# Mixture-of-experts stages: whole fp32 matmuls on unsplit weights, expert pairs in the two column halves of TensorE

## The chip, the cores and the metric

The kernel runs on one core of a Trainium2 chip. The metric is the time of one execution on the device in microseconds (us). Three runs of the kernel before gave 2243.08, 2245.78 and 2247.37 us; the median is 2245.78.

The engines go by the names of the profile: PE is TensorE (PEld its weight loads), DVE is VectorE, ACT is ScalarE, POOL is GpSimd, SP issues most transfers from memory.

## The reference, cut to what matters

A block of two layers comes first (a gated delta rule mixer, then an attention mixer), and behind each mixer stands a mixture of experts over 256 tokens of width 1024. A second block follows, which the change doesn't touch. The part that the change is about:

```
def hier_moe(x, w_grp, b_grp, w_rt, b_rt, w_gate, w_up, w_down):
    ...                                  # softmax over 4 groups, best group; in it the best 2 of 4 experts
    gate = jnp.sum(jax.nn.one_hot(expert_id, MOE_EXPERTS, dtype=jnp.float32) * top_w[..., None], axis=1)
    def step(acc, e_in):
        wg, wu, wd, ge = e_in            # 1024 x 256, 1024 x 256, 256 x 1024, all float32
        hdn = jax.nn.silu(xt @ wg) * (xt @ wu)
...
    y, _ = lax.scan(step, jnp.zeros((b * t, d), jnp.float32), (w_gate, w_up, w_down, gate.T))
```

In the sum over 16 experts a token counts only for the two that it was routed to. Each layer has its own 16 experts, 50.3 MB of weights.

## The kernel before

Activations stand as h: 128 partitions x 8 blocks (kb) x 256 tokens. Weights are one long array W in the order of use; `load` streams it in pieces of 128x1024 (512 KB) into `wraw` buffers (5) through SP. Products are made in fp32r, which needs the operands cut in two: `fill` copies each piece to a rounded high part `wh` (ACT, L161) and subtracts for the low part `wl` (L164, columns up to `s.cut` on DVE, the rest on POOL), and `mm3` (L184 to L186) multiplies high by high, high by low and low by high.

One expert stage, `moe`, runs so. The norm of the mixer ahead ends with transposes of its statistics (L229 on `ln_st`), then writes h and its two parts `xh`, `xl`. Expert 0 is computed for all tokens: `dense_in` with `mm3`, gate and up together, 256 columns each. Meanwhile the router's logits (L832) are formed, DVE works out the routing, and `places` gives each routed token one of CAP = 64 slots in its expert's list. `gather` (L941) multiplies the tokens (`XT`, high and low) by one-hot matrices (`OH`), and leaves each expert's list as 64 columns high and 64 low.

Experts 1 to 15 then go one at a time through a loop: `gate_up` (L1026) holds the list's 128 columns (high, low) in the array and streams the weights' high and low parts, 512 columns each; `hidden` adds the two halves by a matmul with `fold` (L1044) and makes silu(gate) x up; `down` (L1058) does the second product the same way; `combine` (L1072) brings a result back to token order with a selection matrix (`Sel`), 256 columns, and `put_back` adds it to h. At the end `begin` and `end` do expert 0's second product with `mm3` and the last combines, pair by pair, for the norm that follows. `m_cnt` guards a branch (L1087) for lists of over 64 tokens, which isn't taken here.

Around the loop `room` and `again` lend `load` five more buffers of 512 KB (the space of xh and xl, and one tile `more_w`). A scheduler orders the instructions of each engine from the program and its priorities.

## Time and profile before

| | us |
|---|---|
| median of 3 runs | 2245.78 |
| the profiled execution, its own time | 2242.31 |
| its span, first to last instruction | 2240.4 |
| PE busy | 2108.0 (94%) |
| DVE busy | 1563.2 (70%) |
| ACT, POOL busy | 1194.7, 1204.8 |
| expert stage of layer 0, statistics to statistics | 231.64 to 458.68 |
| expert stage of layer 1 | 631.24 to 855.68 |

The span is the profiled execution's time without some 2 us around it. An engine's busy time is a sum over stages of different kinds, so what a change in the expert stages is worth is to be read in these two stretches, which are a fifth of the span.

### The profile page before, as it was taken

To read this page: it belongs to the slowest core of one execution; us is meant where nothing else is said; L and a number is where in the kernel's file an instruction comes from. 1 tells how busy PE (TensorE), PEld (TensorE's weight loads), DVE (VectorE), ACT (ScalarE), POOL (GpSimd) and SP (SyncE) were. 2 spreads that over 40 slices of the span, in tenths; PEclk is the share of its full clock that TensorE was granted. 3 is DMA by queue.
4 is the path that set the end of the run, shared out by engine and by line. 5 is a ranking of instruction groups with operands and counts; after the bars stand their busy time and mean duration, and the time that the engine had idled before them with its cause. 6 is when DMAs were issued, how large, how long until landed. Compare 5 with 4: busy or idle time off the path is not lost.

```text
span 2240.4 us, 43315 instructions
## 1 busy us (share of the span) xinstructions
PE 2108.0 (94%) x16219; PEld 1994.8 (89%) x16219; DVE 1563.2 (70%) x2995; ACT 1194.7 (53%) x2036; POOL 1204.8 (54%) x1100
## 2 busy tenths in 40 slices
PE   8899899889989988999899999999999989999998
PEld 8889777788787777999899999999999988999998
DVE  6856799767779986664788656664665688656654
ACT  6723588556557764444565544444444466545443
POOL 3513466444245655776624367556676644367663
PEclk9999799889989998999999999999999999999999
DMA  5413388553047864555333355555555432355553
GB/s 199 142 37 108 123 284 297 192 182 122 22 146 262 290 236 135 194 175 175 127 104 118 115 175 168 173 176 173 170 178 172 164 109 92 117 184 176 187 186 107
DMA packets 111911, 363.53 MB, mean 162 GB/s; under 512 B 21064, under 2 KB 25160, under 8 KB 111304
## 3 DMA queue, kind: packets, MB, share of 16 engines
q1 hardware_dynamic: 107400, 354.82, 47.7%
q10 hardware_dynamic: 4288, 5.80, 0.8%
q8 instruction: 132, 2.16, 0.4%
q14 instruction: 91, 0.75, 0.1%
HBM read 359.13 MB, written 1.44 MB: 161 GB/s over the span
## 4 chain that ended last, share of the span: by engine, by line
PE 43%; DVE 4%; POOL 2%; ACT 1%; issue 1%; POOLq 0%; DVEq 0%; ACTq 0%
PE bankg L184 13%; PE bankg L185 13%; PE bankg L186 13%; PE bank L1833 2%; PE bank L1757 1%; DVE wl L164 1%; POOL rms_acc L1518 1%; PE bank L1818 1%; ACT wh L161 1%; POOL wl L164 1%; ACT x_p L1741 0%; POOL sq L1516 0%; DVE x_p L1730 0%; DVE x_p L1750 0%; PE bank L1784 0%
## 5 line engine op out<-in xcount | busy, mean ns | idle before, releaser
L164 POOL TENSOR_TENSOR wl<-wraw,wh 128x256 fp32r<-128x256 f32 (+4 forms) x560 | 741.6, 1327 | 603.9 <-ACT wh L161 507.4
L161 ACT ACTIVATE wh<-wraw 128x1024 fp32r<-128x1024 f32 x560 | 590.7, 1058 | 516.9 <-PE bankg L185 260.6
L184 PE MATMUL bankg<-xh,wh 128*128 128x272 f32 (+1 forms) x2624 | 770.0, 294 | 16.0 <-ACT wh L161 7.5
L185 PE MATMUL bankg<-xl,wh 128*128 128x272 f32 (+1 forms) x2624 | 761.3, 290 | 8.1 <-DVE xl L1524 4.3
L186 PE MATMUL bankg<-xh,wl 128*128 128x272 f32 (+1 forms) x2624 | 762.1, 291 | 0.8 <-DVE wl L164 0.7
L164 DVE TENSOR_TENSOR wl<-wraw,wh 128x768 fp32r<-128x768 f32 (+3 forms) x544 | 560.9, 1034 | 267.9 <-ACT wh L161 266.7
L184 PEld LDWEIGHTS bankg<-xh,wh 128*128 128x128 f32 x2624 | 505.2, 193 | 24.8 <-ACT wh L161 7.5
L185 PEld LDWEIGHTS bankg<-xl,wh 128*128 128x128 f32 x2624 | 505.2, 193 | 11.0 <-DVE xl L1524 5.9
L186 PEld LDWEIGHTS bankg<-xh,wl 128*128 128x128 f32 x2624 | 505.5, 193 | 2.1 <-DVE wl L164 1.3
L186 PE MATMUL bankg<-f_hh,wl 128*128 128x272 f32 (+1 forms) x704 | 201.4, 286 | 0.0
L184 PE MATMUL bankg<-f_hh,wh 128*128 128x272 f32 (+1 forms) x704 | 201.2, 286 | 0.0
L185 PE MATMUL bankg<-f_hl,wh 128*128 128x272 f32 (+1 forms) x704 | 200.8, 285 | 0.0
L184 PEld LDWEIGHTS bankg<-f_hh,wh 128*128 128x128 f32 x704 | 132.6, 188 | 0.0
L185 PEld LDWEIGHTS bankg<-f_hl,wh 128*128 128x128 f32 x704 | 132.5, 188 | 0.0
L186 PEld LDWEIGHTS bankg<-f_hh,wl 128*128 128x128 f32 x704 | 132.2, 188 | 0.0
L1574 POOL TENSOR_TENSOR f_g<-f_g,f_u 128x272 f32<-128x272 f32 (+1 forms) x88 | 69.8, 793 | 82.6 <-DVE f_u L1573 80.9
L1573 DVE TENSOR_TENSOR f_u<-bankg,rb 128x272 f32<-128x272 f32 (+1 forms) x88 | 38.4, 437 | 82.3 <-PE bankg L186 82.3
L233 DVE TENSOR_TENSOR f_hl<-f_g,f_hh 128x272 fp32r<-128x272 f32 (+1 forms) x88 | 83.0, 943 | 4.4 <-ACT f_hh L232 4.4
L1026 PE MATMUL bankg<-wl,m_xg 128*128 128x512 f32 x240 | 78.1, 407 | 2.6 <-DVE wl L164 2.4
L1026 PE MATMUL bankg<-wh,m_xg 128*128 128x512 f32 x240 | 79.6, 413 | 0.5 <-DVE m_xg L948 0.5
L164 POOL TENSOR_TENSOR wl<-more_xl,wh 128x320 fp32r<-128x320 f32 x40 | 46.5, 1169 | 30.5 <-ACT wh L161 23.3
L164 POOL TENSOR_TENSOR wl<-more_xh,wh 128x320 fp32r<-128x320 f32 x40 | 45.0, 1126 | 32.8 <-ACT wh L161 29.6
(584 smaller groups left out, 4081.6 us busy)
## 6 DMA issues: line engine op xcount, KB each, us to landing
wraw<-W SPq DMA_DIRECT2D x560, 512.0 KB, 3.6
more_xl<-W SPq DMA_DIRECT2D x40, 512.0 KB, 4.8
more_xh<-W SPq DMA_DIRECT2D x40, 512.0 KB, 4.7
more_w<-W SPq DMA_DIRECT2D x20, 512.0 KB, 6.2
bt<-rpb SPq DMA_DIRECT2D x8, 544.0 KB, 6.3
n_tb<-t ACTq DMA_DIRECT2D x1, 2048.0 KB, 8.1
n_c<-cmp_k ACTq DMA_DIRECT2D x1, 1024.0 KB
n_c<-cmp_v ACTq DMA_DIRECT2D x1, 1024.0 KB
```

What stands on the lines that cost most here:

```text
L161: nc.scalar.activation(wh, r, AF.Copy)
L164: eng.tensor_sub(wl[:, sl], r[:, sl], wh[:, sl].bitcast(F32))
L184: mm(out, wh, xh, start=start, stop=False, **k)
L185: mm(out, wh, xl, start=False, stop=False, **k)
L186: mm(out, wl, xh, start=False, stop=stop, **k)
L233: s.nc.vector.tensor_sub(l, x, h.bitcast(F32))
L1026: PE.matmul(GUs[e], XG[(e - 1) // 4][:, k0 + i, (e - 1) % 4], ws[i][part], start=k0 + i + part == 0, stop=k0 + i + part == KB)
L1518: nc.gpsimd.tensor_add(st["acc"], st["acc"], sq)
L1573: V.tensor_mul(u, pu, rb)
L1574: G.tensor_mul(g, g, u)
L1757: PE.transpose(pt[:96, b * 128:(b + 1) * 128], p[:, b * 96:(b + 1) * 96], s.ident)
L1833: PE.matmul(o[hf * 64:hf * 64 + 64, c * 128:(c + 1) * 128], v(j)[:, b, hf * 64:hf * 64 + 64], st["t"][hf][:, b], start=b == 0, stop=b == 2 ...
```

## The change

- Experts 1 to 14 are taken in pairs (`UNITS`), and 15 by itself. W is arranged so that one piece of 512 KB holds the same 128 rows of both experts' gate and up weights.
- `gate_up` and `down` multiply in whole fp32 and read the pieces as they landed (`raw`); no wh or wl is made for experts. A list is 64 columns of fp32. The two experts of a pair write to PSUM partitions 0 to 63 and 64 to 127, so each uses one half of the array's columns. Expert 15 uses the halves for two parts of its own sum.
- `hidden` transposes instead of folding; `combine` handles both experts of a pair in one product, and the put-back goes by two blocks (512 columns).
- Expert 0 is done in whole fp32 from h itself, both products at the start (`first_down`), its gate is applied on DVE (`first_add`).
- `residual_norm(whole=True)` ahead of an expert stage writes h alone, without xh and xl, and splits no weights meanwhile.
- `load` gets 19 further buffers in an expert stage (the space of xh and xl, the 8 of the wh and wl ring, 7 tiles `more_i`), from its start on; with the 5 of wraw, 24.
- The part of the routing that only the gates need is ordered behind `places`.

The order of instructions at three places. PE, in the loop, one expert before (m_xg is a list, m_gu the gate and up product, m_shd the hidden values, x2 a count):

```order
L1026 MATMUL bankg<-wh,m_xg 128x512 x2
L1026 MATMUL bankg<-wl,m_xg 128x512 x2
L941 MATMUL bank<-m_oh,m_xt 128x256 x4
L1026 MATMUL bankg<-wh,m_xg 128x512 x2
L1026 MATMUL bankg<-wl,m_xg 128x512 x2
L941 MATMUL bank<-m_oh,m_xt 128x256 x4
L1026 MATMUL bankg<-wh,m_xg 128x512 x2
L1026 MATMUL bankg<-wl,m_xg 128x512 x2
L1058 MATMUL bankg<-wh,m_shd 128x512 x2
L1058 MATMUL bankg<-wl,m_shd 128x512 x2
L1058 MATMUL bankg<-wh,m_shd 128x512 x2
L1058 MATMUL bankg<-wl,m_shd 128x512 x2
```

and a pair of experts in the changed kernel (bank and bankg are PSUM tiles, more_ and wraw are stream buffers with a whole weight piece):

```order
L1098 MATMUL bankg<-more_2628,m_xg 64x512 x2
L1098 MATMUL bankg<-more_2629,m_xg 64x512 x2
L1008 MATMUL bank<-m_oh,m_xt 128x256 x8
L1098 MATMUL bankg<-more_2630,m_xg 64x512 x2
L1098 MATMUL bankg<-more_2631,m_xg 64x512 x2
L1008 MATMUL bank<-m_oh,m_xt 128x256 x8
L1098 MATMUL bankg<-more_2632,m_xg 64x512 x2
L1098 MATMUL bankg<-more_2633,m_xg 64x512 x2
L1143 MATMUL bankg<-more_2634,m_shd 64x512
L1143 MATMUL bankg<-wraw,m_shd 64x512
L1143 MATMUL bankg<-more_2634,m_shd 64x512
L1143 MATMUL bankg<-wraw,m_shd 64x512 x5
```

The operand in the array is now 64 columns of fp32, the moving one a piece as it landed, and each piece is used once by each of the two experts; the products of 64 columns alternate with gathers of 128.

PE, where expert 0 ends and the lists begin, before:

```order
L184 MATMUL bankg<-xh,wh 128x256
L185 MATMUL bankg<-xl,wh 128x256
L186 MATMUL bankg<-xh,wl 128x256
L941 MATMUL bank<-m_oh,m_xt 128x256 x17
L1026 MATMUL bankg<-wh,m_xg 128x512 x2
L1026 MATMUL bankg<-wl,m_xg 128x512 x2
L941 MATMUL bank<-m_oh,m_xt 128x256 x7
L1026 MATMUL bankg<-wh,m_xg 128x512 x2
L1026 MATMUL bankg<-wl,m_xg 128x512 x2
```

and changed (m_sg is expert 0's hidden tile, 128x256 products on the pieces more_xh):

```order
L1036 MATMUL bankg<-h,wraw 128x256 x8
L1008 MATMUL bank<-m_oh,m_xt 128x256 x8
L1070 MATMUL bankg<-m_sg,more_xh 128x256 x16
L1008 MATMUL bank<-m_oh,m_xt 128x256 x8
L1098 MATMUL bankg<-more_xl,m_xg 64x512 x4
L1008 MATMUL bank<-m_oh,m_xt 128x256 x8
L1098 MATMUL bankg<-more_wh,m_xg 64x512 x4
L1008 MATMUL bank<-m_oh,m_xt 128x256 x8
L1098 MATMUL bankg<-more_wh,m_xg 64x512 x4
L1098 MATMUL bankg<-more_wl,m_xg 64x512 x4
```

Expert 0's second product now stands between the first gather and the first pair; before, it stood behind the loop.

SP, the loads up to the norm's last basic block (the branch), before:

```order
L142 DMA wraw<-W 128x1024 x9
L142 DMA more_w<-W 128x1024
L142 DMA wraw<-W 128x1024 x4
L351 UNCONDITIONAL_BRANCH x2
L142 DMA wraw<-W 128x1024 x6
L142 DMA more_xl<-W 128x1024
```

and changed (the rows above these are nine wraw, more_2628 and more_2629):

```order
L150 DMA wraw<-W 128x1024 x2
L150 DMA more_2630<-W 128x1024
L150 DMA wraw<-W 128x1024
L150 DMA more_2631<-W 128x1024
L150 DMA more_wh<-W 128x1024
L150 DMA more_wl<-W 128x1024
L150 DMA more_wh<-W 128x1024
L150 DMA more_wl<-W 128x1024
L150 DMA more_wh<-W 128x1024
L150 DMA more_wl<-W 128x1024
L150 DMA more_xh<-W 128x1024
L378 UNCONDITIONAL_BRANCH x2
```

Before, five or six pieces of the expert stage are issued ahead of the branch; now 15 are, each as its buffer comes free, and nine more buffers follow right behind it.

The diff, cut to its core:

```diff
-MCUT = 704
+MORE = 7
...
+UNITS = [(e, e + 1) for e in range(1, 15, 2)] + [(15, 15)]
...
-        s.stops = [2 * c for c in (MOE_AT[0], MOE_AT[0] + 48, MOE_AT[1], MOE_AT[1] + 48, I["W"].shape[0])]
+        s.stops = [2 * c for c in (MOE_AT[0], MOE_AT[1], I["W"].shape[0])]
+        s.spare_to = 0
...
-            elif s.spare:
+            elif s.spare and s.chunk < s.spare_to:
                 (r, back), own = s.spare.pop(0)(), False
...
+    def raw(s):
+        if not s.raws:
+            s.load()
+        r, back, _ = s.raws.pop(0)
+        s.ngroup += 1
+        if back:
+            s.used.append(back)
+        return r
+    def raw_done(s):
+        while s.used:
+            s.used.pop(0)()
+        s.load()
...
-            s.fill(False, 1)
+            if not whole:
+                s.fill(False, 1)
...
-            s.fill(False)
+            if not whole:
+                s.fill(False)
...
-        if meta is None:
+        if meta is None and not whole:
...
-                    if meta is None:
+                    if whole:
+                        A.activation(r[:, kb], y[:, j], AF.Identity, scale=gv, bias=bv)
+                    elif meta is None:
...
+            def ring(tag):
+                s.spare.append(lambda: (s.ring.tile([128, 1024], F32, name="more_" + tag, tag=tag), lambda: ring(tag)))
+            def room(tag):
+                t = s.xp.tile([128, 2, 1024], F32, name="more_" + tag, tag=tag)
+                left = [0, 0]
+                def back():
+                    left.pop()
+                    if not left and s.chunk < s.spare_to:
+                        room(tag)
+                s.spare += [lambda i=i: (t[:, i], back) for i in range(2)]
+            def more(t):
+                s.spare.append(lambda: (t, lambda: more(t)))
+            room("xh")
+            room("xl")
+            for tag in ("wh", "wl"):
+                for _ in range(4):
+                    ring(tag)
+            for i in range(MORE):
+                more(one.tile([128, 1024], F32, name="more_%d" % i))
+            s.load()
...
-            def dense_in(blocks, x, pg, pu):
-                for kb in range(KB):
-                    wh, wl = blocks(4)
-                    for c in range(4):
-                        o = (pg, pu)[c // 2][:, (c % 2) * T:(c % 2 + 1) * T]
-                        sl = slice(c * 128, c * 128 + 128)
-                        s.mm3(o, (wh[:, sl], wl[:, sl]), x(kb), kb == 0 and c % 2 == 0, kb == KB - 1, skip_group_check=True)
-                    if blocks == s.nb and kb % 2:
-                        s.tick()
+            def dense_in(kb, w, x, pg, pu):
+                for c in range(4):
+                    o = (pg, pu)[c // 2][:, (c % 2) * T:(c % 2 + 1) * T]
+                    PE.matmul(o, w[:, c * 128:c * 128 + 128], x, start=kb == 0 and c % 2 == 0, stop=kb == KB - 1,
+                              skip_group_check=True)
...
-            dense_in(s.nb, X, pg, pu)
+            for i in range(4):
+                r = s.raw()
+                for k in range(2):
+                    dense_in(2 * i + k, r[:, k * 512:k * 512 + 512], h[:, 2 * i + k, :T], pg, pu)
+                s.raw_done()
+                s.tick()
...
+            y0 = one.tile([128, KB, T], F32, name="m_y0")
+            def first_down():
+                for i in range(2):
+                    r = s.raw()
+                    for p in range(2):
+                        pd = s.bank(True)
+                        for k in range(2):
+                            for f in range(2):
+                                b = (2 * p + k) * 2 + f
+                                PE.matmul(pd[:, k * T:(k + 1) * T], r[:, b * 128:b * 128 + 128], sg[:, f],
+                                          start=f == 0, stop=f == 1)
+                        m = 4 * i + 2 * p
+                        A.activation(f2(y0[:, m:m + 2]), pd, AF.Copy)
+                    s.raw_done()
...
+            def first_add(pgt):
+                g = gate_rows(gate, 0, pgt)
+                for m in range(0, KB, 2):
+                    V.tensor_mul(y0[:, m:m + 2], y0[:, m:m + 2], g)
+                    V.scalar_tensor_tensor(h[:, m:m + 2, :T], h[:, m:m + 2, :T], ALPHA, y0[:, m:m + 2],
+                                           op0=OP.mult, op1=OP.add)
...
-            def gate_up(e, k0):
-                if k0 == 0:
-                    GUs[e] = s.bank(True)
-                ws = [s.nb(4) for _ in range(2)]
-                for part in range(2):
-                    for i in range(2):
-                        PE.matmul(GUs[e], XG[(e - 1) // 4][:, k0 + i, (e - 1) % 4], ws[i][part], start=k0 + i + part == 0,
-                                  stop=k0 + i + part == KB)
...
+            HV = slice(0, CAP), slice(CAP, 2 * CAP)
+            single = lambda u: UNITS[u][0] == UNITS[u][1]
+            def gate_up(u, i0, i1):
+                if i0 == 0:
+                    GUs[u] = s.bank(True)
+                for i in range(i0, i1):
+                    r = s.raw()
+                    for b in range(2):
+                        e = UNITS[u][b] - 1
+                        kb = 2 * i + b if single(u) else i
+                        PE.matmul(GUs[u][HV[b]], XG[e // 4][:, kb, e % 4], r[:, b * 512:b * 512 + 512],
+                                  start=i == 0, stop=i == (3 if single(u) else 7), skip_group_check=True)
+                    s.raw_done()
...
+            def hidden(u):
...
+                    x = GUs[u][:, c * 128:(c + 1) * 128]
+                    if single(u):
+                        PE.matmul(pt[:, c * w:(c + 1) * w], x, fold, start=True, stop=True)
+                    else:
+                        PE.transpose(pt[:, c * w:(c + 1) * w], x, s.ident)
...
+            def down(u):
                 py = [s.bank(True), s.bank(True)]
-                for f in range(2):
-                    wh, wl = s.nb(8)
-                    for w in (wh, wl):
-                        for b in range(2):
-                            PE.matmul(py[b], HDs[e][:, f], w[:, b * 512:b * 512 + 512], start=f == 0 and w is wh,
-                                      stop=f == 1 and w is wl)
-                gc = gcol[:, e:e + 1]
-                yh, yl = (two.tile([128, 2, 512], F32R, name="m_y" + x, tag="m_y" + x, bufs=4) for x in "hl")
+                for f in range(1 if single(u) else 2):
+                    r = s.raw(), s.raw()
+                    for b in range(2):
+                        for i in range(2):
+                            hd = HDs[u][:, i] if single(u) else HDs[u][:, f, HV[i]]
+                            PE.matmul(py[b][HV[i]], hd, r[i][:, b * 512:b * 512 + 512], start=f == 0,
+                                      stop=single(u) or f == 1, skip_group_check=True)
+                    s.raw_done()
...
+            def combine(ps, u, m, start=True, stop=True):
+                for i in range(2):
+                    PE.matmul(ps, Ys[u][i][:, m * 128:m * 128 + 128], Sel[u], start=start and i == 0,
+                              stop=stop and i == 1, skip_group_check=True)
...
+                for u, p in todo[:n]:
+                    ps = s.bank()
+                    for k in range(2):
+                        combine(ps[:, k * T:(k + 1) * T], u, p + k, k == 0)
+                    V.tensor_add(h[:, p:p + 2, :T], h[:, p:p + 2, :T], ps.rearrange("p (a b) -> p a b", a=2))
...
             with tc.high_priority(offset=200):
-                places()
-            for kb in range(KB):
+                placed = places()
+            first_down()
+            for kb in range(0, KB, 2):
                 gather(0, kb)
-                if kb > 1 and kb % 2:
-                    gate_up(1, kb - 3)
-            gate_up(1, 6)
+                if kb:
+                    gate_up(0, kb - 2, kb)
+            gate_up(0, 6, 8)
...
+            first_add(s.bank())
...
+            for u in range(9):
+                if u < 8:
+                    step = 1 if single(u) else 2
+                    if u:
+                        gate_up(u, 0, step)
+                if u:
+                    hidden(u - 1)
+                    selector(u - 1)
...
+                    down(u - 1)
+                    if u < 7:
+                        todo += [(u - 1, p) for p in range(0, KB, 2)]
...
-                    for f in range(2):
-                        s.mm3(half(m), s.nb(), (hh[:, f], hl[:, f]), m == p and f == 0, False, skip_group_check=True)
-                    combine(half(m), range(13, 15), m, False, False)
+                    combine(half(m), 6, m, m == p, False)
```

## Rows read from the trace of the kernel before

**Rows 1.** The page's head and busy line.

```profile
span 2240.4 us, 43315 instructions
...
PE 2108.0 (94%) x16219; PEld 1994.8 (89%) x16219; DVE 1563.2 (70%) x2995; ACT 1194.7 (53%) x2036; POOL 1204.8 (54%) x1100
```

**Rows 2.** Windows, both stages: length, PE PEld DVE ACT POOL, PEclk, DMA, GB/s.

```profile
231.64:264.68 33.04, 26.26 (x159) 25.22 (x159) 24.49 (x56) 16.99 (x28) 14.36 (x7) 0.71 0.30 96
264.68:279.14 14.46, 12.80 (x91) 11.43 (x89) 13.67 (x17) 8.17 (x11) 9.71 (x5) 0.85 0.71 255
279.14:433.40 154.26, 139.90 (x775) 115.75 (x775) 148.81 (x204) 121.24 (x170) 96.66 (x84) 0.96 0.80 280
433.40:458.68 25.28, 19.61 (x124) 18.77 (x122) 9.53 (x20) 5.61 (x8) 1.70 (x6) 0.77 0.19 64
631.24:663.00 31.76, 26.12 (x159) 25.14 (x159) 24.62 (x56) 17.85 (x29) 14.70 (x7) 0.71 0.32 102
663.00:677.92 14.92, 13.01 (x90) 11.66 (x89) 13.70 (x17) 8.12 (x11) 9.68 (x5) 0.84 0.69 247
677.92:832.50 154.58, 140.16 (x776) 116.05 (x776) 148.74 (x204) 121.25 (x170) 96.27 (x84) 0.96 0.80 279
832.50:855.68 23.18, 18.21 (x124) 17.29 (x122) 9.80 (x20) 5.49 (x8) 1.52 (x3) 0.87 0.01 3
```

**Rows 3.** Windows of the subtractions (L164) alone, layer 0's loop: DVE, then POOL.

```profile
279.14:433.40 154.26, 98.17 (x85) 96.66 (x84) 0.96 0.80 280
```

**Rows 4.** Waits of PE, layer 0's loop: waiter, releaser, total us, times, longest.

```profile
PE bankg L1058 <- DVE m_yl L1064: 7.7, 3, 3.7
```

**Rows 5.** Timeline, layer 0's stage, its start: start, us, engine, line, count.

```profile
234.97 0.80 PE L184 MATMUL bankg<-xh,wh 128*128 128x256 f32 x2 [1.66 <-ACT xh L367]
...
240.86 0.28 PE L184 MATMUL bankg<-xh,wh 128*128 128x256 f32 x1
...
244.69 3.36 PE L832 MATMUL bank<-m_wr,h 128*128 128x20 f32 x28
...
250.04 4.72 POOL L164 TENSOR_TENSOR wl<-wraw,wh 128x1024 fp32r<-128x1024 f32 x2 [2.93 <-DVE m_xt L233]
...
250.19 2.30 DVE L839 TENSOR_TENSOR m_e1o<-m_e1o,c_iota 128x40 f32<-128x40 f32 x1
...
259.01 0.58 PE L887 MATMUL bank<-m_mask,c_tri 128*128 128x16 f32 x2 [4.82 <-issue]
```

**Rows 6.** Windows, a stretch in which the weight stream runs at its fastest.

```profile
320.00:330.00 10.00, 10.00 (x62) 8.64 (x62) 10.00 (x16) 8.54 (x13) 6.38 (x6) 1.00 0.97 347
```

**Rows 7.** Timeline of PE, fp32r products in the loop.

```profile
412.05 0.28 PE L1072 MATMUL bank<-m_sel,m_yh 128*128 128x256 f32 x1
412.17 0.28 PE L1072 MATMUL bank<-m_sel,m_yl 128*128 128x256 f32 x1
...
414.42 0.63 PE L1058 MATMUL bankg<-wh,m_shd 128*128 128x512 f32 x2
414.89 0.63 PE L1058 MATMUL bankg<-wl,m_shd 128*128 128x512 f32 x2
```

**Rows 8.** Timeline of PE, whole fp32 products over all 128 columns (first mixer).

```profile
119.41 3.75 PE L594 MATMUL bank<-Tbd,g_q 128*128 128x128 f32 x32
```

**Rows 9.** Timeline of PE, fp32 products in 64-column halves (attention of layer 1).

```profile
549.02 1.04 PE L1432 MATMUL bank<-n_pt,n_vt 128*64 128x128 f32 x16
550.00 0.39 PE L184 MATMUL bankg<-xh,wh 128*128 128x256 f32 x1
```

**Rows 10.** Windows, 120 to 130 us, in the stretch of rows 8.

```profile
120.00:130.00 10.00, 10.00 (x92) 10.00 (x91) 5.98 (x10) 3.32 (x7) 0.00 (x0) 1.00 0.15 48
```

**Rows 11.** Timeline of DVE, the first of the last accumulations into h.

```profile
445.56 0.69 DVE L282 SCALAR_TENSOR_TENSOR h<-h,bankg 128x512 f32<-128x512 f32 x1 [10.44 <-PE bankg L1072]
```

**Rows 12.** Lines: an expert's result scaled by its gate (DVE), busy total and mean.

```profile
L1064 DVE SCALAR_TENSOR_TENSOR m_yl<-bankg,m_gcol,m_yh 128x512 fp32r<-128x512 f32 x29 | 20.3, 740 | 1.3 <-ACT m_yh L1063 1.3
```

**Rows 13.** Weight loads of line L1432: min/median/max in ns, first and last start.

```profile
L1432 PEld LDWEIGHTS bank<-n_pt,n_vt x192: 132/137/232, 542.5 to 608.2; 128*64 128x64 f32 x192
```

More of the change, by code (lines that the diff above doesn't have):

```diff
@@ L880, in moe @@
             OH = one.tile([128, 2, 16, CAP], F32R, name="m_oh", tag="m_oh")
-            gcol = one.tile([128, 16], F32, name="m_gcol")
+            OH15 = one.tile([128, 2, 2 * CAP], F32R, name="m_oh15")
+            gcol = one.tile([128, 8], F32, name="m_gcol")
             cnt = one.tile([1, 1], I32, name="m_cnt")
@@ L990, in moe @@
             sg = one.tile([128, 2, T], F32, name="m_sg", tag="m_sg")
-            hh = one.tile([128, 2, T], F32R, name="m_hh")
-            hl = one.tile([128, 2, T], F32R, name="m_hl")
             dense_hidden(sg, pg, pu)
-            def room(tag):
-                t = s.xp.tile([128, 2, 1024], F32, name="more_" + tag, tag=tag)
-                left = [0, 0]
-                def back():
-                    left.pop()
-                    if not left and s.wide:
-                        room(tag)
-                s.spare += [lambda i=i: (t[:, i], back) for i in range(2)]
@@ L1007, in moe @@
-            s.wide = True
-            room("xh")
-            room("xl")
-            more = one.tile([128, 1024], F32, name="more_w")
-            def again():
-                if s.wide:
-                    s.spare.append(lambda: (more, again))
-            again()
-            GUs, HDs, Ys, Sel = {}, {}, {}, {}
-            def gate_up(e, k0):
-                if k0 == 0:
-                    GUs[e] = s.bank(True)
-                ws = [s.nb(4) for _ in range(2)]
-                for part in range(2):
-                    for i in range(2):
-                        PE.matmul(GUs[e], XG[(e - 1) // 4][:, k0 + i, (e - 1) % 4], ws[i][part], start=k0 + i + part == 0,
-                                  stop=k0 + i + part == KB)
@@ new lines, in hidden @@
+                V.tensor_mul(hd, sg, v(2))
+                HDs[u] = hd
+            def down(u):
+                py = [s.bank(True), s.bank(True)]
+                for f in range(1 if single(u) else 2):
[6 more added lines that the diff above has]
+                    s.raw_done()
+                gc = gcol[:, u:u + 1]
+                yh, yl = (two.tile([128, 2, 512], F32R, name="m_y" + x) for x in "hl")
@@ L1102, in overflowed @@
[L1102 to L1120 removed]
+                xs = two.tile([128, KB, T], F32, name="o_x", tag="m_xg")
@@ new lines, in overflowed @@
+                for kb in range(KB):
+                    for part in range(2):
+                        for t in range(2):
+                            o = part * T + t * 128
+                            PE.transpose(pgt[:, o:o + 128], XT[:, t, part, kb * 128:(kb + 1) * 128].bitcast(F32), s.ident)
+                    A.activation(xs[:, kb], pgt[:, :T], AF.Copy)
+                    V.tensor_add(xs[:, kb], xs[:, kb], pgt[:, T:])
+                w = one.tile([128, 512], F32, name="o_w", tag="m_oh")
@@ L1121, in overflowed, with blocks @@
+                so = one.tile([128, 2, T], F32, name="o_s", tag="m_sg")
+                def blocks(b0):
+                    A.dma_start(w, s.W[first + b0 // 16][:, (b0 % 16) * 128:(b0 % 16) * 128 + 512])
+                for e in range(1, 16):
+                    for kb in range(KB):
+                        blocks(MOE_GU[e][kb])
+                        dense_in(kb, w, xs[:, kb], pg, pu)
                     dense_hidden(so, pg, pu)
                     V.tensor_mul(so, so, gate_rows(gover, e, pgt))
-                    s.split(so, *ho)
@@ L1141, in moe @@
+            with tc.issue_after(placed.ins):
+                late[0]()
             s.split(gate, gs[:, :, :, 0], gs[:, :, :, 1])
             V.scalar_tensor_tensor(gover, posm, float(CAP), gate, op0=OP.is_ge, op1=OP.mult)
-            for e in range(1, 16):
-                slot_gate(e)
+            for u in range(8):
+                slot_gate(u)
             slot_gates_out()
-            V.tensor_mul(sg, sg, gate_rows(gate, 0, s.bank()))
-            s.split(sg, hh, hl)
-            s.cut = MCUT
+            first_add(s.bank())
```

213 lines of the change are left out of this document (96 added, 117 removed).

## The prediction, on record before the changed kernel ran

> **What bounds the kernel now.** I read the page first, then windows over the two expert stages, then what waits inside them. The page says that PE is busy for 2108.0 of a span of 2240.4 us [rows 1]: a stage gets shorter only where PE works less or waits less. The windows cut each expert stage into four stretches: A, from the statistics to the first gather; B, up to where the gathers and gates are done; C, the loop; D, the end [rows 2]. The stages last 227.0 and 224.4 us, and the reader is to see that each stretch has another limit.
>
> In C (154.26 us in layer 0) DVE is busy for 148.81 us, PE for 139.90 [rows 2], and 98.17 of DVE's are the subtractions for low parts of weights (POOL has 96.66 more) [rows 3]. So DVE sets the loop's pace, PE is near behind, and PE's waits name DVE [rows 4]. In A PE works for 26.26 of 33.04 us, at a mean clock of 0.71 [rows 2]: it starts 3.3 us in, runs at half speed until about 240.86, and later waits 4.82 us for the routing. Meanwhile POOL subtracts a piece in 2.4 us (4.72 for two), and a tiny DVE operation of 40 elements beside it takes 2.30 [rows 5]; its neighbours of the same size take about 0.2, and three of them are stretched so. The stream moves 280 GB/s in the loop at a DMA share of 0.80, but only 96 in A [rows 2]; where it has buffers it does 347 [rows 6], which is 1.51 us for a piece of 524,288 bytes. 96 pieces per layer are 145 us: the stream is no bound at 227 us, but isn't far from one in a stage of 175.
>
> **Prices.** A fp32r product of 256 columns takes a slot of 0.12 us (412.05 to 412.17), one of 512 columns 0.235 (two in 414.42 to 414.89) [rows 7]. A whole fp32 product is recorded as two passes. Over 128 columns of the array a pass with 128 moving ones takes 0.112 to 0.117 (3.75 us for 32) [rows 8]. In 64-column halves 16 such records take 549.02 to 550.00, 0.98 us [rows 9]: one after another they would need 1.8, so the two halves run at the same time, eight slots of 0.109 and about 0.1 for the change from 64 to 128 columns. This scales to 0.218 for a pass of 256 and 0.436 for one of 512, so **a pair of 512-column products, one in each half, costs 2 x 0.436 = 0.872 us**. That is the disputed price: its bounds are 0.87 (fully side by side) and 1.74 (one after another); I take the lower end, by the row that it is nearest to in form. Such a stretch holds its clock: 120 to 130 us, whole fp32 products, shows PEclk 1.00 [rows 10].
>
> **Stretch A.** Splits and low parts go; POOL's subtractions, which stretch the routing, go with them. PE: 3.3 us to the first product as before; 32 products of 256 columns in 64 passes x 0.218 = 13.95; the slow clock at the start, 5.9 us at half speed, so 2.9 lost [rows 5]; 16 transposes x 0.109 = 1.7; logits, 32 passes x 0.115 = 3.6 (28 take 3.2 now, 244.69 to 247.88); masks 1.1. The routing behind the logits took 11.1 us to the masks at 259.01 [rows 5], less three stretches of some 2.1 it is 4.8; 4.1 us of dense products and transposes lie beside it, so 0.7 remains as a wait (bounds 0, and 4.8 if nothing covers it). Sum 27.3 to 27.4, against 33.04 and 31.76: **-5.6 and -4.4**.
>
> **Stretch B.** Expert 0's second product moves here: 32 passes x 0.218 = 7.0. Gathers, 32 x 0.12 = 3.8 and 16 more, 1.9. The first pair's gate and up product, 8 x 0.872 = 7.0. Six changes between 64 and 128 columns, 0.6. Slot gates and gate rows, some 20 small slots, 2.3. A wait for expert 0's hidden tile, 1.0 (bounds 0 and 2). Sum 23.5, against 14.46 and 14.92: **+9.0 and +8.6**. Expert 0's additions on DVE (eight operations) have the first pair as cover; without it they cost 8 x 0.7, since h is needed again only by the put-backs.
>
> **Stretch C.** The order shows what is left per pair: 16 gate and up products, 8 down, gathers and combines between them. For PE: gate and up 52 x 0.872 = 45.3; down 30 x 0.872 = 26.2; gathers 80 x 0.12 = 9.6 (0.1175 in the longer rows: 9.4); combines 96 x 0.12 = 11.5; transposes and the fold, some 50 x 0.11 = 5.6; 58 changes of width x 0.1 = 5.8. That is 103.8 us of work. The same arithmetic gives 129.7 for the loop of before, which took 154.26, so 24.6 were waits, gaps and slow clock; the slow clock at its start took some 4.9, which leaves 19.7. DVE loses 98.17 of 148.81 us and keeps about 50 [rows 2, 3], POOL nearly all, ACT its copies; so nobody but PE is near 100 us. How much of the waits stays is unknown: 0 if they all came from DVE's backlog, 19.7 if they come from the chains (product, hidden, down, scaling). I take 5, since the largest named wait is for an operation that stood behind subtractions [rows 4]. 108.8, against 154.26 and 154.58: **-45.5 and -45.8**.
>
> The stream must feed this. From the statistics to the loop are now 50.9 us, in which 34 pieces land at 1.51 us, and 14 are used. The loop uses 82 in 108.8 us, in which 72 land. 20 + 72 is 92: ten to spare, and 24 buffers hold that lead. That cover costs nothing while the rate stays above about 310 GB/s (1.70 us a piece: 30 - 14 + 64 = 80).
>
> **Stretch D.** Expert 0's second product is gone. Now 12.2 us pass from the loop's end (433.40) to the first of the last additions (445.56) [rows 2, 11]; afterwards the last expert's scaling (about three steps of 0.74 [rows 12], 2.4 with handovers) and a combine of 0.8 come there, and the rest stays as it is: 13.1 + 3.2 = 16.3 in layer 0, 12.9 + 3.2 = 16.1 in layer 1. **-9.0 and -7.1**.
>
> **Sum.** Layer 0: -5.6 + 9.0 - 45.5 - 9.0 = -51.1. Layer 1: -4.4 + 8.6 - 45.8 - 7.1 = -48.7. Together -99.8. The profiled execution had 2242.31 us, 2 over its span and 0.2% under the median of 2245.78. 2242.3 - 99.8 = **2142 us**. Nothing takes it back in the next stage: its weights come once buffers are free, as before, and the DMA is nearly idle in D (64 and 3 GB/s [rows 2]).
>
> **Rivals.**
> *The waits stay.* Hidden values and scalings are a chain of PE, ACT, DVE and PE again, and pairs make it longer, with fewer links. If all 19.7 us stay, each layer is 14.7 longer: 2171. For it: PE's waits for the scaling, 7.7 us in three [rows 4]. Against it: DVE was over 96% busy then. Chance 0.13.
> *The stream becomes the bound.* If it keeps the loop's 280 GB/s (1.87 us a piece), 27 land before the loop, 13 are left, 58 more come: 11 short, 20.6 us per layer, 2183. Against it: 347 with buffers [rows 6], and share 0.80 says that buffers were wanting. Chance 0.12.
> *Weight loads lie bare.* Each pass needs its own load, of 137 ns for 64 columns [rows 13]. If a load waits until the other half's pass is through, 90 pairs x 2 passes x 0.137 = 24.7 us per layer: 2192. The eight slots of 0.109 leave no room for loads of 0.137 in between [rows 9, 13], so the trace speaks against it. Chance 0.05.
> The Trainium skill ("TensorE: Matmul & The Clock Gate", Part 3, "What overlaps and what doesn't") says that a weight load overlaps running products only where its row group differs; two column halves have all rows in common, so by that rule this rival would hold. The trace of the halves disagrees with it, at least for 128 moving columns.
> *Slower: the halves don't run side by side* when each streams 512 columns of a different piece. Then 90 pairs cost 0.872 more: 78.5 us per layer, 2142 + 157 = 2299. It decides from 1.43 us a pair on (99.8 / 180 = 0.55 above 0.872). Against it stand only short streams [rows 9]. Chance 0.05.
> *Slower too: the clock.* If the loop ran at 1.2 GHz, its 103.8 us would double: about 2350. The loop had 0.96 [rows 2], fp32 stretches 1.00 [rows 10]. Chance 0.02.
>
> **Numbers.** The likeliest case has 0.62; 0.01 is left for no change. Its own range: without any wait of those taken (5 in C, 1 in B, 0.7 in A per layer) and without the slow start 2142 - 19 = 2123, and with half of the rivals' waits 2157. The range 2118 to 2190 takes in the waits and the stream and leaves out the rarer ones. Faster by over 0.2% (about what a measurement of this kernel can tell from no change): 0.62 + 0.13 + 0.12 + 0.05 = 0.92; the same 0.01; slower 0.07.
>
> **What would show it.** Right: the loop at 105 to 115 us with PE busy for over 90% of it at clock near 1.00, DVE near 50; starts of the 64x512 products in twos, 0.44 apart from the next two; A near 27 with the masks some 5 us behind the logits; B near 23.5; D near 16; no wait of the 64x512 products for a DMA. Wrong: starts 0.44 apart one by one (the halves take turns), gaps of 0.14 between passes (weight loads), waits for pieces late in the loop (stream), waits for scaled results before the combines (chain), or a PEclk of half in the loop.

## The result, and the profile after

Four runs of the changed kernel took 2145.5 to 2152.95 us, median 2149.76, against 2245.7 before: a ratio of 0.9577 (95% interval 0.9557 to 0.9596). The forecast was 2142 in a range of 2118 to 2190. The profiled execution took 2147.22 us with a span of 2145.4.

The page's head and busy line of the changed kernel, which answers to [rows 1]: PE, DVE, ACT and POOL all work less, and PE's share of the span is still the largest.

```profile
span 2145.4 us, 40943 instructions
...
PE 2042.1 (95%) x15675; PEld 1845.1 (86%) x15675; DVE 1312.2 (61%) x2727; ACT 966.0 (45%) x1732; POOL 963.2 (45%) x908
```

The windows of its two expert stages, A to D in each, with the columns of [rows 2]:

```profile
233.37:259.56 26.19, 24.59 (x126) 21.51 (x127) 13.20 (x46) 8.75 (x15) 0.00 (x0) 0.82 0.64 250
259.56:284.33 24.77, 24.77 (x140) 16.59 (x139) 8.79 (x21) 5.13 (x10) 0.00 (x0) 1.00 0.66 232
284.33:389.00 104.67, 104.13 (x550) 47.84 (x548) 39.43 (x75) 20.16 (x35) 0.00 (x0) 1.00 0.82 307
389.00:409.59 20.59, 10.80 (x61) 9.56 (x59) 9.88 (x20) 5.62 (x9) 1.73 (x6) 0.77 0.45 164
581.38:611.06 29.68, 24.66 (x126) 21.52 (x127) 13.30 (x46) 9.59 (x16) 0.00 (x0) 0.78 0.68 242
611.06:635.80 24.74, 24.74 (x140) 16.59 (x138) 8.77 (x21) 5.13 (x10) 0.00 (x0) 1.00 0.65 233
635.80:740.50 104.70, 104.16 (x550) 47.85 (x548) 39.46 (x75) 20.16 (x35) 0.00 (x0) 1.00 0.82 305
740.50:761.63 21.13, 10.72 (x60) 9.48 (x59) 10.15 (x20) 5.52 (x9) 1.58 (x3) 0.76 0.16 61
```

In the loop PE is busy for 104.13 of 104.67 us at a clock of 1.00, DVE for 39, POOL not at all: the bound has gone from DVE to PE.

The boundary between B and C in these rows doesn't lie where [rows 2] have it. There C begins with the loop's first products for gate and up (279.14); here it begins behind them, with the first transposes of hidden values. PE's timeline at the boundary, and the two windows of layer 0 with C begun as in [rows 2]:

```profile
280.40 2.13 PE L1008 MATMUL bank<-m_oh,m_xt 128*128 128x256 f32 x16
282.46 1.94 PE L1098 MATMUL bankg<-more_wl,m_xg 128*64 128x512 f32 x8
284.33 0.66 PE L1128 MATMUL bank<-c_ident,m_gu 128*128 128x128 f32 x4
```

```profile
259.56:282.46 22.90, 22.90 (x132) 16.10 (x130) 6.92 (x18) 4.54 (x9) 0.00 (x0) 1.00 0.65 223
282.46:389.00 106.54, 106.00 (x557) 48.32 (x556) 41.30 (x78) 20.76 (x36) 0.00 (x0) 1.00 0.82 307
```

Layer 1 gives the same 22.9 and 106.5 (boundary at 633.96). Measured against the forecast with this boundary, in us:

| stretch | forecast, layers 0 and 1 | measured |
|---|---|---|
| A | 27.4, 27.4 | 26.2, 29.7 |
| B | 23.5, 23.5 | 22.9, 22.9 |
| C | 108.8, 108.8 | 106.5, 106.5 |
| D | 16.3, 16.1 | 20.6, 21.1 |
| change of the stage | -51.1, -48.7 | -50.8, -44.2 |

The rest of the program is unchanged in sum (+1.7 ahead of the first stage, -0.8 between the two, -0.9 behind the second): -95.0 in the span. What asks for an explanation is D in both layers, A in layer 1, and why C needed almost none of the waits that were granted to it. The experiments below count the loop from the first transposes on, 104.7 us in the changed kernel.

The timeline of PE in the loop, where a pair's second product begins (start, us, count):

```profile
292.89 0.59 PE L1143 MATMUL bankg<-more,m_shd 128*64 128x512 f32 x1
292.89 0.59 PE L1143 MATMUL bankg<-wraw,m_shd 128*64 128x512 f32 x1
293.31 0.59 PE L1143 MATMUL bankg<-more,m_shd 128*64 128x512 f32 x1
293.32 0.59 PE L1143 MATMUL bankg<-wraw,m_shd 128*64 128x512 f32 x1
```

Each start comes in twos, one for each half, and the next two follow 0.43 us later: a pair costs 0.86 us, at the lower end of the bounds. The wait list of PE in this loop has one line, where [rows 4] had 7.7 us for one releaser alone:

```profile
PE bankg L1143 <- DVE m_shd L1133: 0.5, 1, 0.5
```

PE's weight loads for the pairs (min/median/max in ns) last as long as those of [rows 13]:

```profile
L1098 PEld LDWEIGHTS bankg<-more,m_xg x176: 132/137/137, 285.1 to 731.2; 128*64 128x64 f32 x176
```

With PE busy all the time and starts 0.43 us apart they lie wholly beside the other products. The rule that the forecast cited from the Trainium skill ("TensorE: Matmul & The Clock Gate", Part 3, "What overlaps and what doesn't": a load overlaps only where the row group differs) doesn't hold for these column halves.

In D, PE's timeline shows where it stands still:

```profile
390.24 0.29 PE L1156 MATMUL bankg<-m_sel,m_yl 128*128 128x256 f32 x1
395.63 0.55 PE L1156 MATMUL bank<-m_sel,m_yh 128*128 128x256 f32 x1 [5.10 <-PEq L1172]
395.98 0.41 PE L1156 MATMUL bank<-m_sel,m_yl 128*128 128x256 f32 x1
396.19 0.41 PE L1156 MATMUL bank<-m_sel,m_yh 128*128 128x256 f32 x1
```

L1172 is the branch for lists of over 64 tokens: 5.10 us of idle time (5.45 in layer 1), and slots of 0.21 us instead of 0.12 afterwards, at a granted clock of 0.50 up to 399.8. And at the start of layer 1's stage the timeline of ACT shows what the norm's last step waits behind:

```profile
581.88 0.34 ACTq L100 DMA_DIRECT2D c_slots<-slots  x1
584.71 0.33 ACTq L100 DMA_DIRECT2D c_slotp<-slotp  x1
585.08 0.44 ACTq L100 DMA_DIRECT2D c_fold<-fold  x1
585.56 1.28 ACT L104 ACT_TABLE_LOAD   x1 [6.28 <-DMA c_slots<-slots]
586.85 1.58 ACT L394 ACTIVATE h<-ln_y,c_vecs 128x256 f32<-128x256 f32 x3
```

ACT issues small constant loads there. Each issue lasts 0.33 to 0.44 us, but from the start of one (581.88) to that of the next (584.71) 2.8 us pass. And h, without which no product starts, comes only at 586.85, 5.5 us after the statistics.

### The profile page after: what moved, and what is told of

Read it like the earlier page. It is cut to its first block, busy times and chain, and to the rows that moved or that the text cites. A ratio compares the mean times of both kernels' runs of the same rounds, so it can differ in the third digit from the quotient of the medians.

```text
span 2145.4 us, 40943 instructions
## 1 busy us (share of the span) xinstructions
PE 2042.1 (95%) x15675; PEld 1845.1 (86%) x15675; DVE 1312.2 (61%) x2727; ACT 966.0 (45%) x1732; POOL 963.2 (45%) x908
## 4 chain that ended last, share of the span: by engine, by line
PE 45%; DVE 3%; POOL 2%; ACT 1%; issue 1%; POOLq 0%; DVEq 0%; ACTq 0%
PE bankg L207 14%; PE bankg L208 13%; PE bankg L209 13%; PE bank L1910 2%; PE bank L1834 1%; DVE wl L172 1%; PE bank L1895 1%; POOL rms_acc L1595 1%; ACT wh L169 1%; POOL wl L172 1%; POOL sq L1593 0%; ACT x_p L1818 0%; DVE x_p L1807 0%; PE bank L1861 0%; DVE xl L1601 0%
## 5 line engine op out<-in xcount | busy, mean ns | idle before, releaser
L172 POOL TENSOR_TENSOR wl<-wraw,wh 128x256 fp32r<-128x256 f32 (+2 forms) x468 | 614.7, 1315 | 518.2 <-ACT wh L169 443.3
L207 PE MATMUL bankg<-xh,wh 128*128 128x272 f32 (+1 forms) x2560 | 747.4, 292 | 12.0 <-ACT wh L169 6.9
L208 PE MATMUL bankg<-xl,wh 128*128 128x272 f32 (+1 forms) x2560 | 740.0, 289 | 8.1 <-DVE xl L1601 4.2
L209 PE MATMUL bankg<-xh,wl 128*128 128x272 f32 (+1 forms) x2560 | 739.6, 289 | 1.0 <-DVE wl L172 0.9
L169 ACT ACTIVATE wh<-wraw 128x1024 fp32r<-128x1024 f32 x468 | 494.7, 1058 | 510.2 <-PE bankg L208 259.4
L172 DVE TENSOR_TENSOR wl<-wraw,wh 128x768 fp32r<-128x768 f32 (+2 forms) x468 | 480.3, 1027 | 267.0 <-ACT wh L169 264.6
L207 PEld LDWEIGHTS bankg<-xh,wh 128*128 128x128 f32 x2560 | 489.3, 191 | 20.2 <-ACT wh L169 6.9
L208 PEld LDWEIGHTS bankg<-xl,wh 128*128 128x128 f32 x2560 | 489.1, 191 | 10.9 <-DVE xl L1601 5.9
L209 PEld LDWEIGHTS bankg<-xh,wl 128*128 128x128 f32 x2560 | 489.3, 191 | 2.3 <-DVE wl L172 1.5
L1164 DVE TENSOR_TENSOR h<-h,bank 128x512 f32<-128x512 f32 x48 | 31.9, 686 | 66.0 <-PE bank L1156 66.0
L1156 PEld LDWEIGHTS bank<-m_sel,m_yh 128*128 128x128 f32 x120 | 24.2, 202 | 40.3 <-issue 33.6
```

Source lines behind the costliest of these rows:

```text
L169: nc.scalar.activation(wh, r, AF.Copy)
L172: eng.tensor_sub(wl[:, sl], r[:, sl], wh[:, sl].bitcast(F32))
L207: mm(out, wh, xh, start=start, stop=False, **k)
L208: mm(out, wh, xl, start=False, stop=False, **k)
L209: mm(out, wl, xh, start=False, stop=stop, **k)
L1156: PE.matmul(ps, Ys[u][i][:, m * 128:m * 128 + 128], Sel[u], start=start and i == 0, stop=stop and i == 1, skip_group_check=True)
```

## The experiments

Twelve kernels ran. All edits are to the changed kernel, except where the kernel before is named.

**1. No branch.** The call is dropped.

```diff
             begin(0)
-            overflow()
```

> Leaves out the branch for lists of over 64 tokens (no token's result changes with these inputs). Theory: stretch D came out 4.3 to 5.0 us per layer longer than forecast because PE stands still for 5.1 and 5.45 us at this branch, with nothing of expert 0 left to lie beside it, and then starts at the slow clock. Then D falls from 20.6 and 21.1 us to 14 to 16 in each layer, and the whole by 10 to 14 us to about 2137. Rival: D is the chain of combine, addition and statistics, and the branch lies beside it; then D falls by under 2 us per layer and the whole stays within 4 us of 2150.

Median 2138.89 (ratio 0.9532, 0.9515 to 0.9548), 10.9 us less. Its windows of D:

```profile
389.82:404.77 14.95, 8.97 (x52) 7.81 (x50) 9.87 (x20) 5.65 (x9) 1.73 (x6) 0.81 0.75 276
736.71:750.77 14.06, 8.35 (x52) 7.14 (x50) 10.05 (x20) 5.51 (x9) 1.58 (x3) 0.88 0.19 71
```

D is 5.6 and 7.1 us shorter, so the branch stands on the path, and without it D lies 1.3 and 2.0 us under the forecast. The dropped call is more than the jump: it also loads the count into a register of four engines, and it is a border that the scheduler moves no instruction across. The experiment measures all of it together.

**2. The branch of the kernel before.** The same edit to the kernel before; the question is whether the branch had been hidden there.

> The kernel before the change without its branch for long lists (left out; no result changes with these inputs). Theory (cover): there PE stood still for only 2.1 and 1.2 us at the branch, so leaving it out gives 3 to 5 us in all, against 10.9 in the changed kernel: 2239 to 2242. Rival: the branch costs the same in both, about 11 us, and the forecast missed D for another reason: 2233 or less.

Median 2231.61 (2223.49 to 2235.78; ratio 0.994, 0.9917 to 0.9963), 12.3 us less than the 2243.91 of its chip. The windows of D:

```profile
435.75:453.11 17.36, 14.67 (x118) 14.10 (x117) 9.89 (x21) 5.60 (x8) 1.70 (x6) 0.98 0.24 79
828.38:845.96 17.58, 14.66 (x118) 14.09 (x116) 10.12 (x21) 5.49 (x8) 1.51 (x3) 0.97 0.00 1
```

From 25.3 and 23.2 (loop's end to statistics) D falls to 17.4 and 17.6. A part of that is only moved: without the border, products of expert 0 stand ahead of the loop's end, some 0.5 us of work. Whole stages are the safer measure. They are 5.3 and 6.3 us shorter here (221.7 and 218.2 against 227.0 and 224.4), and 5.8 and 6.1 in experiment 1 (170.4 and 174.1 against 176.2 and 180.2). The theory of a lost cover falls: the branch cost as much before as after, though PE's longest single wait there was 2.1 us:

```profile
438.68 0.51 PE L1072 MATMUL bankg<-m_sel,m_yh 128*128 128x256 f32 x1 [2.13 <-PEq L1087]
438.99 0.42 PE L1072 MATMUL bankg<-m_sel,m_yl 128*128 128x256 f32 x1
439.20 0.41 PE L184 MATMUL bank<-m_hh,wh 128*128 128x256 f32 x1
```

The rest was spread: the clock (0.77 and 0.87 in D of [rows 2], 0.98 and 0.97 here) and the delays behind it. Of the slow clock in D of layer 0, the part behind the wait (438.68 to 445.5, granted 0.50) follows the branch. Another part (from 431.69 to 435.3) began ahead of it and is gone here too, with another order of the products around it; how much of the gain is due to that order no run separates.

**3. An earlier branch.** It stands ahead of the last expert's hidden values, behind 16 passes that wait for nothing.

```diff
             for u in range(9):
+                if u == 8:
+                    overflow()
...
             begin(0)
-            overflow()
```

> The branch for long lists stands before the last expert's hidden values instead of behind its second product. Theory: PE's sequencer takes 3.3 to 4.8 us for the branch in every kernel, the one of before included; what differs is the cover. Before, it came to the branch 2.6 us before the products that it had issued were through; now it comes there as they end. Ahead of the new place stand 16 passes of 512 columns (3.4 us) that wait for nothing, so the sequencer can run ahead and PE's wait falls from 5.1 and 5.45 us to 1.5 to 3, without the slow clock behind it or with less of it: D and C together 3 to 5 us less per layer, the whole 2140 to 2144. Rival: the sequencer cannot pass products that aren't through, so the wait stays at 5 us at any place, and the whole at 2150.

Median 2151.15 (0.9576 to 0.9606): no gain. PE's sequencer did run ahead, as the instructions of the branch's line show (count, duration in ns, first and last start):

```profile
L1172 PEldq COMPARE_BRANCH  x2: 3514/3548/3582, 381.8 to 733.3; - x2
L1172 ACTq COMPARE_BRANCH  x2: 45/48/50, 385.3 to 736.9; - x2
...
L1172 ACTq EVENT_SEMAPHORE  x2: 17/17/17, 388.4 to 741.8; - x2
```

PE's jump, 3.5 us from 381.8 on, lay beside its last products. But ACT came to its own branch at 385.3 and did its next instruction at 388.4, and PE's next product started at 388.52, 4.21 us idle with ACT's queue as releaser. In sum the rival's time came, though not by its reason: D fell to 15.0 and 14.3 us, C rose to 110.8 and 113.5. ACT pays for the branch too: from its branch to its next instruction it took 2.4 to 5.4 us in the twelve kernels that have the branch. Hiding PE's share bares ACT's. DVE went on after 0.2 and 0.6 us in the changed kernel, so not every engine pays.

**4. Nothing else on the DMA queues while the branch is taken.** First the next stage's loads were held by program order alone, behind a small transfer that depends on h:

```diff
+            if s.hold and s.chunk >= s.spare_to:
+                break
...
                 yield end(2)
+                nc.sync.dma_start(one.tile([128, 1], F32, name="m_hold"), h[:, 2, :1])
+                s.hold = False
+                s.load()
```

> Keeps the branch, and holds the next stage's first loads on SP until an addition behind the branch is done. Theory: the code behind the branch has to be brought by the DMA engines (their queues for instructions show packets there), and before the change these were idle at that point while now the weight stream runs at 300 GB/s and more; then PE's wait at the branch falls from 5.1 and 5.45 us to about the 2.1 of before, D by about 3 us per layer, and the whole to about 2144. Rival: the branch costs 5 us wherever PE has no work in its queue; then the wait stays at 5.1 to 5.5 us and the whole at 2150 or later by what the held loads miss.

The hold failed: four loads still went out ahead of that transfer, at 385.6 to 391.4, and 135 GB/s moved during the branch. Median 2148.53, waits 4.78 and 4.04 us. With the transfer and the six loads behind it kept in program order:

> The same trial as the held stream, now so that the next stage's first four or five loads on SP really stand behind an addition that follows the branch (before, they had still gone out ahead of it, and the DMA engines were as busy during the wait as without the edit). Theory: PE's wait at the branch is the time in which the code behind it is brought by the DMA engines; with these idle it falls from 4.0 to 5.6 us (six waits measured so far with the stream running) to the 2.1 to 2.5 of before the change, D falls by 2 to 3 us per layer, and the whole by 4 to 6 us to about 2145. Rival: the wait is that of a jump when PE's queue is empty, whatever the DMA engines do; then it stays between 4 and 5.6 us and the whole at 2150.

Median 2147.9 (0.9548 to 0.9584). Now 10 GB/s moved, and the jump on PE's sequencer, of this kernel, of the changed one, and of the hold that failed:

```profile
L1180 PEldq COMPARE_BRANCH  x2: 3448/3568/3687, 389.4 to 742.7; - x2
```

```profile
L1172 PEldq COMPARE_BRANCH  x2: 4262/4492/4722, 391.1 to 742.4; - x2
```

```profile
L1176 PEldq COMPARE_BRANCH  x2: 3302/3615/3928, 392.9 to 746.6; - x2
```

PE's waits were 4.34 and 4.38 us, D 19.4 and 20.2. Against the changed kernel the jump is about 1 us shorter, but the stream is not shown to be the reason: with the hold that failed it took 3.30 us while 135 GB/s moved. Over all runs the jump took 3.3 to 4.0 us in the twelve cases with up to 75 GB/s (the kernel before: 3.33 and 3.96) and 3.3 to 6.0 in the twelve with over 90. So 3.3 to 4.0 us stay without the stream, and what lengthens some of the others is open. The theory had said 2 to 3 us, so the rival is nearer. And the stretch between the two expert stages, whose loads came late, took 175.0 us instead of 171.8, which is more than D gained.

**5. Constants from POOL.** Seven lines like this one:

```diff
-            slots = s.const("slots", [128, CAP], one, A)
+            slots = s.const("slots", [128, CAP], one, G)
```

> Issues the seven small constant loads of an expert stage from POOL instead of ACT. Theory: in layer 1 the first product of expert 0 came 6.1 us after the statistics (2.7 in layer 0) because ACT issues these loads there, each slower beside the weight stream, ahead of the norm's last step; then stretch A of layer 1 falls from 29.7 to about 26.3 us, layer 0 stays at 26.2, and the whole falls by 3 to 4 us. Rival: the norm in layer 1 waits for something else, or the constants then come too late for the routing; then A of layer 1 stays above 28 us, with the wait at the masks.

Median 2145.83 (0.956, 0.9544 to 0.9576). That lies within the interval of the changed kernel, but the stretch is plain in its windows of A:

```profile
234.24:259.72 25.48, 23.52 (x127) 20.58 (x127) 13.21 (x46) 10.04 (x16) 0.00 (x0) 0.87 0.67 258
580.92:606.50 25.58, 23.98 (x127) 21.00 (x127) 13.20 (x46) 10.04 (x16) 2.06 (x4) 0.87 0.74 284
```

Layer 1's A is 4.1 us shorter and equal to layer 0's: the theory holds, and nothing waits for the constants later.

**6. Two edits together**, held loads or early branch with the constants from POOL:

> Both edits together: loads held behind the branch, and the small constants issued from POOL. Theory: they touch different stretches (D in both layers, A in layer 1), so their gains add, 4 to 6 us and 3 to 4 us: 2140 to 2143, the fastest version that keeps the branch. Rival: the held loads cost the next stage what D gains; then only the 4 us of the constants remain, about 2146.

> The early branch, and the small constants issued from POOL. Theory: the gains add (3 to 5 us per layer, and 4 us in layer 1): 2136 to 2140, the fastest so far that keeps the branch. Rival, if the branch costs the same at any place: 2146, as with the constants alone.

2147.44 (2146.27 to 2152.59) and 2149.68 (2147.47 to 2153.17). In the first the two stages are 7.5 us shorter than in the changed kernel (349.0 against 356.5), and the stretch between them is 5.7 longer (177.5 against 171.8), as its rival said. In the second, D is 5.6 and 6.6 us shorter and the loop 8.5 and 7.7 longer than in the changed kernel, as with the early branch alone; A of layer 1 keeps its gain (25.5). Neither beats the constants alone.

**7. Halves by twos and by fours.** The same products, first two (then four) in a row for one half. Of the first edit, the lines for the second product:

```diff
-                    for b in range(2):
-                        for i in range(2):
+                    for i in range(2):
+                        for b in range(2):
```

> Same products, in another order: two products for one half of the columns, then two for the other, instead of one by one. Theory: the halves run at the same time only where products that follow each other go to different halves. Then a group of four products (eight passes) takes six to seven slots of 0.43 us instead of four; there are 41 such groups in a loop and 4 before it, so each layer gets 39 to 58 us longer and the whole 2225 to 2265. Rival: each half has its own queue; then nothing changes, 2150. The rival of the forecast by which halves cannot run side by side would show no change either, but with starts 0.43 us apart one by one in the changed kernel, which its trace does not have.

The loop took 105.8 us instead of 104.7 (the whole 2157.68 in one run), with starts in twos as before:

```profile
295.40 0.59 PE L1144 MATMUL bankg<-more,m_shd 128*64 128x512 f32 x1
295.45 0.59 PE L1144 MATMUL bankg<-wraw,m_shd 128*64 128x512 f32 x1
```

The second start now comes 0.05 us behind the first, not 0.01 or less. The trace lists products by their start and so doesn't show the order in which they were issued; if that is the order of the edit, the halves aren't served in it, and the rival holds.

> Second product of a pair: four products (eight passes) for one half of the columns, then four for the other. By twos nothing had changed (loop 105.8 against 104.7 us). If each half has a queue that reaches over eight passes, nothing changes again: loop 105 to 107. If it reaches over four only, part of each group runs alone: with 7 groups, up to 7 x 8 x 0.43 = 24 us more when nothing overlaps, so 112 to 129 us for the loop.

Second products in groups of eight passes: the loop took 117.1 us, 12.4 more (the whole 2175.06 in one run). One group in PE's timeline:

```profile
291.47 1.88 PE L1144 MATMUL bankg<-more,m_shd 128*64 128x512 f32 x4
293.19 2.37 PE L1144 MATMUL bankg<-wraw,m_shd 128*64 128x512 f32 x9
295.39 0.59 PE L1144 MATMUL bankg<-wraw,m_shd 128*64 128x512 f32 x1
295.82 0.59 PE L1144 MATMUL bankg<-wraw,m_shd 128*64 128x512 f32 x1
296.25 0.59 PE L1144 MATMUL bankg<-wraw,m_shd 128*64 128x512 f32 x1
```

The first four passes run alone, 0.43 us apart, the next four of either half side by side, the last four alone: 12 slots for what takes 8 one by one. Seven groups x 4 x 0.43 = 12.0, nearly all of the 12.4. So the other half is reached over four passes, and not over eight.

**8. Fewer stream buffers.** `MORE = 0` leaves 17; without the wh and wl ring, too, nine are left.

> 17 stream buffers instead of 24 (without the seven extra tiles). By the forecast's arithmetic of the stream: the loop uses 82 pieces in 104.7 us, the last of them some 3 us before its end. With 17 full buffers at its start 65 pieces are left, 98 us at 1.51 us each, against 101.7: no wait, or a few us where pieces are late in bursts. Expected 0 to 3 us per layer, 2150 to 2156. Rival: the stream is already the bound in places and 24 are needed; then waits for pieces appear in the loop, with 10 us per layer or more.

2151.21 us in one run; the loop took 105.9, 1.2 more, with no wait for a piece in PE's list.

> Nine stream buffers (the five of wraw and the space of xh and xl). By the same arithmetic 73 pieces are left when the loop begins, 110 us at 1.51 us each against 101.7: 9 us of waits in the loop of each layer, 5 to 16 with bursts, 2160 to 2182. Rival: a piece that is freed late also stops the stream, as before the change, where it ran at 280 GB/s in the loop; then 73 pieces take 137 us and each layer gets 35 us longer, 2220.

2180.6 us in one run. The loop took 118.9 and 120.2 us. Its window in layer 0:

```profile
283.27:402.13 118.86, 113.00 (x550) 47.84 (x548) 38.93 (x75) 19.41 (x35) 0.00 (x0) 1.00 0.95 340
```

DMA share 0.95 at 340 GB/s, against 0.82 and 307 with 24 buffers: the stream is near its fastest ([rows 6]), and the 14 to 16 us per layer lie in what the arithmetic allowed (9, with 5 to 16 for bursts). The waits for pieces by which it came to that don't show, though. PE's whole wait list of this loop names no DMA:

```profile
PE bank L1153 <- ACT m_yh L1146: 2.8, 5, 0.8
PE bank L1125 <- ACT m_gu L1101: 1.5, 2, 0.8
PE bank L1123 <- ACT m_gu L1101: 0.8, 1, 0.8
PE bankg L1140 <- DVE m_yl L1147: 0.7, 1, 0.7
```

Of the 14.2 us more in layer 0, 5.3 are idle time of PE and 8.9 are busy time (113.0 against 104.1) for the same 550 products. The scheduler put them in another order with fewer buffers: in PE's timeline they change 94 times between 64 and 128 columns, 56 times in the changed kernel. What the buffers are worth is shown, about 1 us per layer for the seven extra tiles and some 13 for the eight of the ring. That the loop waits for the stream is not.

## Why the prediction was right, and where it was not

**The price of a pair** (0.872) was right: 0.86. So the forecast's slower side had no part in it: no clock of 1.2 GHz, bare weight load or wait for the stream appeared in the loop either.

**The waits in C** were mis-sized: 5 us were granted, 0.5 came. The work was mis-sized the other way: PE was busy for 106.0 us against 103.8 forecast, so C is only 2.3 under it. The chains of hidden values and scalings are still there, yet the 19.7 us of the kernel before vanished with DVE busy for 39 us instead of 149. That DVE's backlog made them fits this, but no run put the backlog back, and a pair also gives a chain more of PE's work as cover (some 14 us, where one expert had 10).

**Stretch B** came out 0.6 us shorter in both layers. PE was busy for all of its 22.9 us, so the wait of 1.0 that the forecast granted for expert 0's hidden tile didn't come.

**Stretch A** has the right mechanism and a missing term in layer 1: seven transfers that ACT issues ahead of the norm's last step. Before, their starts in layer 1 lay 0.4 to 0.5 us apart, with 161 GB/s on the DMA queues (627 to 631); now the stage's own pieces go out at that time, 390 to 419 GB/s move (578 to 585.5), and up to 2.8 us lie between two starts. Experiment 5 took this away: 25.6 us. That the early loads are what stretches the issues fits the rates, but no run held them back there. The forecast followed them on SP alone.

**Stretch D** is the step that failed: "Now 12.2 us pass from the loop's end (433.40) to the first of the last additions (445.56)", and afterwards 2.4 for scaling and 0.8 for a combine. It charged all of the 12.2 to expert 0's second product and gave the branch no term; the longest wait there names it with 2.1 us only. Yet 8.7 of the 12.2 us ran at half the clock (433.4 to 435.3 and 438.7 to 445.5), and 2.1 more PE stood still. Experiments 1 and 2 separate branch and product: without the branch in either kernel, D is 17.4 and 17.6 before, 15.0 and 14.1 after. The removal is worth 2.4 and 3.5 us there, some 0.5 more with the work that moved out of D, not 9.0 and 7.1. The branch costs 5.3 to 6.3 us per stage in both kernels and stayed.

The Trainium skill ("Runtime: NRT & Kernel Launch", Instruction fetch mechanics) says that a taken branch to code outside what has been fetched stalls until that code has been brought. The durations fit that: 3.3 to 4.8 us on PE's sequencer in all twelve kernels with the branch (once 6.0 in the one with nine buffers, where 176 GB/s moved during it), and 3.1 and 4.9 us on ACT in experiment 3. That the time goes into bringing code no run shows. Taken as a rule while reading the kernel, it would have asked for a price for a branch that "isn't taken": its body is jumped over.

In sum the misses of -2.3 per layer in C, -1.2 and +2.3 in A, -0.6 per layer in B, +4.3 and +5.0 in D give +4.7: -95.1 instead of -99.8. The median lies 2.5 us over the profiled execution. That the whole came so near is in part luck: D alone was forecast 9.3 us too short, and 5.8 of that are made up by B and C, which were forecast too long.

## What to carry to other kernels

Before a stretch's time is charged to the work that a change removes, take what else lies in it apart, a jump over rarely used code above all: here it cost 5.3 to 6.3 us per stage, it held PE's sequencer for 3.3 to 6.0 us and ACT for 2.4 to 5.4, and a wait list shows only what is bare at one engine. Whoever starts a stream earlier should look at every queue that issues anything at that time, not only at the one that carries the stream. Where a stage's boundaries are compared between two kernels, the same instruction should stand at both. Two products of 64 columns each ran side by side in fp32 at the price of one here, also where the program gives one half four passes in a row, and no longer when it gives it eight.

## What was not expected of the hardware

Column halves overlap by a reach of four passes: groups of four passes changed the loop by 1.1 us, groups of eight by 12.4. A jump on PE's sequencer took 3.3 to 4.8 us in 23 of 24 cases, at both places where it was tried, and 3.3 to 4.0 us of that stay with little on the DMA queues. Between the starts of two small transfers issued on ACT lay up to 2.8 us while 390 GB/s moved, and 0.4 to 0.5 us at 161 GB/s.
